# Seventh convolution pair moved into the in-projection's second part, with the work around the seam re-placed

## The chip, the cores and the metric

One core of a Trainium2 chip runs the program once. The metric is the device time of that run in microseconds (us).

## The reference, cut to what matters

One decoder layer on 1024 tokens of width 1024, all in float32. The change is inside the in-projection and what feeds on it:

```python
h = rms_norm(x, g_mix)
z = h @ w_in + b_in                              # 1024 -> 7168 columns
va, ga, xb, gb, sa, sb = split(z)                # 1024, 1024, 1536, 1536, 1024, 1024
u = causal_depthwise_conv(va * sigmoid(ga), conv_a_w, conv_a_b)     # width 31
y_a = silu(layer_norm(u)) @ w_a_out
v = rg_lru(causal_depthwise_conv(xb, conv_b_w, conv_b_b), ...)      # h[t] = a[t]*h[t-1] + b[t]
y_b = (v * gelu(gb)) @ w_b_out
x = x + (sigmoid(sa) * y_a + sigmoid(sb) * y_b) @ w_o
```

Then follow a squared-ReLU MLP and a last norm, which the change does not touch.

## The kernel before, in words

Every matmul is 128x128 by 128x512. To keep float32 accuracy each operand is split into a high part (rounded to the fast format) and a low part (what is left), and three products high*high, high*low, low*high are summed. The in-projection's 56 column chunks of 128 are done in two parts.

**First part (slots).** The list `CH` (line 704) holds 26 chunks: all 12 of `xb` and the pairs `va`/`ga` numbers 0 to 6. The loop over slots `s` (line 829) computes one chunk in each: 8 k-tiles x 3 products x 2 token halves = 48 matmuls (`chunk_mm`, L743). In between stand the small head matmuls `rg` (L550 to L552) of the recurrence's gates. Their results pass ScalarE as a sigmoid (L560) into head tiles `g15_0`, `g15_1`, and SyncE (SP) copies a third of the last head of each group of four into three gate tiles, `g0_9` to `g0_11` and `g1_9` to `g1_11` for the last group (L565). ScalarE then takes `exp` and `tanh` of each tile (`scan_exp`, L576 and L577) and a slot later a square root (`scan_root`, L584). [...] After the roots VectorE runs `scan_tile(t)` (L593 to L596): a scale, a one-column fill, a product and the recurrence scan itself; SP stores the result to `hd`.

**Second part (steps).** The remaining chunks are done in pairs by a seven-product scheme (Strassen-Winograd): two column blocks, two k halves, two token halves, and products numbered 1 to 7 over sums and differences of weights and of tokens. A product is 12 matmuls (`z_mm`, L944), a pair 84. `ZPAIRS` (line 747) lists the 15 pairs, `zseq` the order of the products; the first twelve steps are (pair, product) = (0,1) (1,1) (0,2) (1,2) (0,6) (0,7) (1,7) (0,5) (1,6) (0,3) (0,4) (1,5). Each product needs

- a weight operand `zo{pair}_{product}`, high and low, made four steps ahead (`z_lhs`): either ScalarE writes the high part and VectorE subtracts for the low part (products 5 and 7), or ScalarE writes the negated source, GpSimd (POOL) lets a DMA add the source to it for the low part, and ScalarE writes the high part (`split_dma`, L65 to L67); its source is a raw weight tile `zw` or a sum `zs` that VectorE makes;
- a token operand. Products 1 to 3 take the tokens of the first part. Products 4 to 7 take differences of token blocks: `x_load(c2)` reads the four blocks of k half `c2` back from DRAM, `x_sum(c2)` makes four subtractions on VectorE, `x_parts(c2, p)` splits the result for product `p` into `xs{p}h_{c2}` and `xs{p}l_{c2}`.

In each step the third matmul is the first that uses the low part of the weight operand. I call the border between the two parts the joint: the first matmul of step 0.

**Order.** All engines run their instructions in the order of the code inside `manual_schedule`; nothing is reordered. `later()` collects VectorE work of a slot or step and `vector_work` (line 718) sorts it by a modelled ready time and fills gaps with taps of the width-31 convolution (`conv`, L655) as far as a modelled clock allows. The dictionaries `XS` (line 818) and `ZX` (line 1036) say which token work stands in which slot or step. SP's DMA issues also stand in program order, and an issue that waits holds up all behind it.

Of the kernel before, what the change touches and what calls it, by code (L numbers as in the profile page):

```python
# [30 lines left out]
def trunk_kernel(ctx: ExitStack, tc: tile.TileContext, x, xt_in, xt_eo, vecs, w_in, w_a_out, w_b_pl, w_b_sq,  # L31
# [413 lines left out]
    VA, GA, XB, GB, SA, SB = 0, 8, 16, 28, 40, 48  # L445
# [121 lines left out]
    at_, rooted = {}, {}  # L567
# [23 lines left out]
    def scan_tile(t):  # L591
# [4 lines left out]
        nc.vector.tensor_tensor_scan(i, a, i, 0.0, ALU.mult, ALU.add)  # L596
        nc.sync.dma_start(hd[t], i)

    ut = {}
    yd = dp.tile([8, P, S], F32, name="yd")  # L600
    ysum = []
# [7 lines left out]
    def u_mul(j, ps, ready=0):  # L609
        uv = ut[j].rearrange("p (o n) -> p o n", o=2)  # L610
        later(ready, 1.28, nc.vector.scalar_tensor_tensor, uv, ps.rearrange("p (n o) -> p o n", o=2),
              bin_c[:, VA + j:VA + j + 1], uv, ALU.add, ALU.mult)
        fresh.append(j)
# [88 lines left out]
                      ALU.subtract)  # L702

    CH = [XB, VA, GA, XB + 1, XB + 2, VA + 1, GA + 1, XB + 3, XB + 4, XB + 5, VA + 2, GA + 2]
    CH += [XB + t for t in range(6, 12)] + [c for j in range(3, 7) for c in (VA + j, GA + j)]
    NU = 7
    CH[-2:] = CH[:-3:-1]
    NC1 = len(CH)
    zps = {n: z0[n] for n in range(N0)}
# [3 lines left out]
    def later(ready, cost, f, *a):  # L713

        todo.append((ready, len(todo), cost, f, a))

    def vector_work(end):
        for ready, _, cost, f, a in sorted(todo, key=lambda x: x[:2]):
            dve(cost, ready, f, *a)
        todo.clear()  # L720
        taps["wait"] += fresh
        fresh.clear()
        fill(end)
# [20 lines left out]
                                 start=n == 0, stop=n == 23)  # L744
        at("P", len(halves) * (n1 - n0) * MM)

    ZPAIRS = [GB + 2 * i for i in range(6)] + [VA + 7] + [SA + 2 * i for i in range(4)]
    ZPAIRS += [SB + 2 * i for i in range(4)]
    NZ = len(ZPAIRS)
    zraw, zs, zo, zb = {}, {}, {}, {}  # L750
    zn = [0]

    def z_load(i, kk):

        zraw[i, kk] = raw = qp.tile([P, 2, 4, P], F32, tag="p", name=f"zw{i}_{kk}", bufs=4)
        c = ZPAIRS[i]
        if c < GA:
# [51 lines left out]
    def z_get(n, f):  # L809
        return f(*zseq[n]) if 0 <= n < len(zseq) else None  # L810
# [4 lines left out]
    head_at = {s: n for n, s in enumerate(HS0)}  # L815

    EXP = {head_slot: g for g, head_slot in enumerate(HS0[4 * g + 3] + 1 for g in range(4))}
    XS = {NC1 - 5: ((x_load, 0),), NC1 - 4: ((x_sum, 0),), NC1 - 3: ((x_load, 1), (x_parts, 0, 6)),
          NC1 - 2: ((x_sum, 1), (x_parts, 0, 7, 5)), NC1 - 1: ((x_parts, 0, 4), (x_parts, 1, 6))}
    made = []  # L820
    head_w(0)
    w_load(3)
# [4 lines left out]
    with tc.manual_schedule(engines=ENGINES):  # L827
        for s in range(3, NC1):
# [30 lines left out]
            c = CH[s - 1]  # L859
# [27 lines left out]
            for d in range(5):  # L887
                if s - d in EXP:
# [6 lines left out]
                    t = 3 * g + d - (2 if g < 3 else 1)  # L895
                    if 3 * g <= t < 3 * g + 3:
                        later(rooted[t], 4.8, scan_tile, t)
            if s == NC1 - 1:
                z_get(0, z_lhs)
                z_get(1, z_lhs)  # L900
            for f, *a in XS.get(s, ()):
                f(*a)
# [48 lines left out]
    def z_u(i, j, m_, hf, src):  # L951

        if m_ and hf:
            return
        if (m_, hf) == (0, 0):
            uz[j] = T(f"u{j}")
        d = halved(uz[j], hf)
        if m_ == 0:
            nc.scalar.activation(d, src.rearrange("p (n o) -> p o n", o=2), AF.Sigmoid,
                                 bias=bin_c[:, GA + j:GA + j + 1])  # L960
            ready = at("A", 0.62)
            if hf == 0:
                return
            src = zb[i, "c"]
        else:
            ready = 0
        later(ready, 0.74, nc.vector.scalar_tensor_tensor, d,
              src.rearrange("p (n o) -> p o n", o=2), bin_c[:, VA + j:VA + j + 1], d,
              ALU.add, ALU.mult)
        if hf:  # L970
            ut[j] = uz.pop(j)
            fresh.append(j)

    def z_out(i, m_, hf, src, name):
        if ZPAIRS[i] < GA:
            z_u(i, ZPAIRS[i] - VA, m_, hf, src)
            return
        ci = ZPAIRS[i] + m_
        bias = bin_c[:, ci:ci + 1]
        if ci < SA:  # L980
            t = ci - GB
            h = hb.pop((t, hf))
            a = src if name else EV(f"ze{i}{m_}{hf}")
            nc.scalar.activation(a, src, AF.Gelu_apprx_tanh, bias=bias)

            def mult():
                nc.vector.tensor_tensor(h, h, a, ALU.mult)
                nc.sync.dma_start(hgd[t, :, HALVES[hf]], h)

            later(at("A", 0.62), 0.63, mult)  # L990
        else:
            b, j = divmod(ci - SA, 8)

            g = EV(f"zg{i}{m_}{hf}").rearrange("p (o n) -> p o n", o=2)
            nc.scalar.activation(g, src.rearrange("p (n o) -> p o n", o=2), AF.Sigmoid, bias=bias)
            at("A", 0.62)
            nc.sync.dma_start(halved(spill[b, j], hf), g)
# [35 lines left out]
        elif p == 4:  # L1033
            z_out(i, 1, 0, zb[i, "u"], "c")

    ZX = {0: ((x_parts, 1, 7),), 2: ((x_parts, 1, 5),), 4: ((x_parts, 1, 4),)}
    H_AT = {2: (0, 0), 5: (1, 1), 3: (0, 1), 4: (1, 0)}
    with tc.manual_schedule(engines=ENGINES):

# [118 lines left out]
        def b_post(i, x):  # L1158
# [16 lines left out]
            elif x == "11":  # L1175
# [4 lines left out]
        L = len(zseq)  # L1180
        ZX.update({L - 16: ((a_load, 0),), L - 13: ((a_sums, 0), (hb_load, 0, 0)),
                   L - 12: ((a_parts, 0, "a"), (hb_load, 0, 1)), L - 11: ((a_parts, 0, "s"), (hb_load, 1, 1)),
# [11 lines left out]
        z_get(3, z_lhs)  # L1194
        u_mul(NU - 1, zps[NC1 - 1])
        vector_work(clk["V"])
        z_h(0, 0, 0)
        for n in range(len(zseq) + 2):
            for f, *a in ZL.get(n, ()):
                f(*a)  # L1200
            if n >= L:
                for f, *a in ZX.get(n, ()):
                    f(*a)
# [4 lines left out]
            if n + 3 < len(zseq):  # L1208
                i, p = zseq[n + 3]
# [6 lines left out]
            if n < L:  # L1216
                for f, *a in ZX.get(n, ()):
                    f(*a)
# [751 lines left out]
    with tc.manual_schedule(engines={mybir.EngineType.Activation, mybir.EngineType.DVE,  # L1970
                                     mybir.EngineType.PE}):
        for n in range(len(useq)):
# [4 lines left out]
            while ready < min(len(useq), n + look + 1):  # L1977
                i, p = useq[ready]
# [316 lines left out]
```

## Time and profile before

| what | us |
|---|---|
| median of 3 runs (range) | 1529.34 (1529.16 to 1529.37) |
| the profiled execution | 1528.49 |
| its span on the core | 1526.7 |
| PE busy in the span | 1517.1 |
| VectorE, ScalarE busy | 1200.7, 928.1 |

The span runs from the first to the last instruction and is 1.8 us shorter than the execution's own time. PE is TensorE's matmul engine, DVE VectorE, ACT ScalarE, POOL GpSimd, SPq SyncE's queue of DMA issues. A row of the timeline has the start from the span's begin, the duration, engine, line, operation and tiles without their numbers; in square brackets stands the idle time before it and who ended it.

### The profile page before, as it was taken

To read this page: it belongs to the slowest core of one execution; us is meant where nothing else is said; L and a number is where in the kernel's file an instruction comes from. 1 tells how busy PE (TensorE), PEld (TensorE's weight loads), DVE (VectorE), ACT (ScalarE), POOL (GpSimd) and SP (SyncE) were. 2 spreads that over 40 slices of the span, in tenths; PEclk is the share of its full clock that TensorE was granted. 3 is DMA by queue.
4 is the path that set the end of the run, shared out by engine and by line. 5 is a ranking of instruction groups with operands and counts; after the bars stand their busy time and mean duration, and the time that the engine had idled before them with its cause. 6 is when DMAs were issued, how large, how long until landed. Compare 5 with 4: busy or idle time off the path is not lost.

```text
span 1526.7 us, 18955 instructions
## 1 busy us (share of the span) xinstructions
PE 1517.1 (99%) x6712; PEld 1248.3 (82%) x6712; DVE 1200.7 (79%) x1640; ACT 928.1 (61%) x1299; POOL 190.7 (12%) x228
## 2 busy tenths in 40 slices
PE   9999999999999999999999999999999999999998
PEld 7878887888888888888888888888888888888886
DVE  6999996999999997788769879755555387777777
ACT  6748688576566667645475777554444455545475
POOL 0111011022222222000022322000000000101010
PEclk9999999999999999999999999999999999999999
DMA  8757778698997789964779897333333974776464
GB/s 352 192 135 165 178 179 187 199 262 211 266 254 179 182 207 277 304 216 120 268 197 302 191 213 174 124 127 111 111 111 111 308 264 125 181 206 171 106 124 152
DMA packets 130911, 295.48 MB, mean 194 GB/s; under 512 B 12800, under 2 KB 34944, under 8 KB 130816
## 3 DMA queue, kind: packets, MB, share of 16 engines
q1 hardware_dynamic: 98960, 214.83, 41.5%
q0 software_dynamic: 31568, 78.92, 27.4%
q8 instruction: 52, 0.85, 0.2%
q10 hardware_dynamic: 288, 0.52, 0.1%
q14 instruction: 43, 0.35, 0.1%
HBM read 148.74 MB, written 60.82 MB: 137 GB/s over the span
## 4 chain that ended last, share of the span: by engine, by line
PE 99%; DMA 0%; DVE 0%; ACT 0%; SPq 0%; issue 0%
PE z L743 16%; PE d2b L2015 2%; PE d1b L2015 2%; PE d0b L2015 2%; PE z L273 2%; PE d3b L2015 2%; PE d0e L2015 1%; PE d3e L2015 1%; PE d3a L2015 1%; PE d2e L2015 1%; PE d1e L2015 1%; PE d1a L2015 1%; PE d0a L2015 1%; PE d2a L2015 1%; PE rg L550 1%; PE rg L552 1%
## 5 line engine op out<-in xcount | busy, mean ns | idle before, releaser
L743 PE MATMUL z<-xh,win_h 128*128 128x512 f32 x368 | 115.4, 391 | 0.0
L743 PE MATMUL z<-xl,win_h 128*128 128x512 f32 x368 | 114.9, 390 | 0.0
L655 DVE SCALAR_TENSOR_TENSOR y<-u,vec,y 128x511 f32<-128x511 f32 (+14 forms) x120 | 88.7, 739 | 0.0
L743 PE MATMUL z<-xh,win_l 128*128 128x512 f32 x368 | 87.5, 389 | 0.0
L655 DVE SCALAR_TENSOR_TENSOR yt<-u,vec,yt 128x511 f32<-128x511 f32 (+6 forms) x112 | 82.9, 740 | 0.0
L655 DVE SCALAR_TENSOR_TENSOR y<-yt,csum,y 128x511 f32<-128x511 f32 (+6 forms) x112 | 82.9, 740 | 0.0
L743 PEld LDWEIGHTS z<-xh,win_h 128*128 128x128 f32 x368 | 69.1, 188 | 16.0 <-ACT win_h L67 0.4
L743 PEld LDWEIGHTS z<-xl,win_h 128*128 128x128 f32 x368 | 69.1, 188 | 14.9
L743 PEld LDWEIGHTS z<-xh,win_l 128*128 128x128 f32 x368 | 69.1, 188 | 14.6
L560 ACT ACTIVATE g<-rg,vec 96x1024 f32<-96x1024 f32 x32 | 35.5, 1111 | 72.7 <-PE rg L552 72.7
L1710 ACT ACTIVATE o<-s 128x512 fp32r<-128x512 f32 x56 | 33.8, 624 | 45.2 <-DVE s L1694 26.4
L66 POOL DMA_DIRECT2D zo<-zw x45 | 38.9, 864 | 133.7 <-ACT zo L65 118.4
L501 DVE SCALAR_TENSOR_TENSOR v<-xb,vec,v 128x1023 f32<-128x1023 f32 (+2 forms) x36 | 46.2, 1282 | 4.4 <-ACT v L492 3.5
L66 POOL DMA_DIRECT2D db_10l<-br x4 | 3.5, 868 | 338.3 <-DMA br<-in_w_dram 253.1
L66 POOL DMA_DIRECT2D win_l<-win_raw x23 | 19.8, 861 | 190.6 <-ACT win_l L65 161.9
L65 ACT ACTIVATE zo<-zw 128x512 fp32r<-128x512 f32 x45 | 28.2, 627 | 24.3 <-PE z10f L944 2.1
L1234 DVE TENSOR_TENSOR o<-s,o 128x512 fp32r<-128x512 f32 x56 | 37.3, 684 | 1.5 <-ACT o L1710 1.5
L66 POOL DMA_DIRECT2D zo<-zs x30 | 26.1, 871 | 75.8 <-ACT zo L65 63.8
L67 ACT ACTIVATE zo<-zw 128x512 fp32r<-128x512 f32 x45 | 28.0, 622 | 0.0
L596 DVE TENSOR_TENSOR_SCAN g<-a,g 128x1024 f32<-128x1024 f32 x12 | 27.5, 2292 | 0.4
L66 POOL DMA_DIRECT2D ga<-gsa x8 | 6.9, 866 | 161.2 <-DMA m<-mbd 150.9
L1234 DVE TENSOR_TENSOR o<-w_raw,o 128x512 fp32r<-128x512 f32 x38 | 25.9, 685 | 0.0
(3178 smaller groups left out, 4908.2 us busy)
## 6 DMA issues: line engine op xcount, KB each, us to landing
w_raw<-in_w_dram SPq DMA_DIRECT2D x32, 512.0 KB, 5.5
br<-in_w_dram SPq DMA_DIRECT2D x32, 512.0 KB, 5.6
ar<-fd SPq DMA_DIRECT2D x32, 512.0 KB, 6.9
zw<-in_w_in_dram SPq DMA_DIRECT2D x28, 512.0 KB, 6.9
win_raw<-in_w_in_dram SPq DMA_DIRECT2D x23, 512.0 KB, 4.8
win_l<-win_raw POOLq DMA_DIRECT2D x23, 512.0 KB, 5.1
zo<-zw POOLq DMA_DIRECT2D x45, 256.0 KB, 5.7
gates<-zg SPq DMA_DIRECT2D x32, 256.0 KB, 4.5
```

Of the source, the lines that this page charges most:

```text
L65: nc.scalar.activation(l, src, AF.Copy, scale=-1.0)
L66: nc.gpsimd.dma_start(l, src, accum_op=ALU.add)
L67: nc.scalar.activation(h, src, AF.Copy)
L273: nc.tensor.matmul(z0[i][:, HALVES[hf]], w0[i][w][:, k, :], xpart(a, hf, k), start=k == 0 and which == "hh", stop=k == 7 and which == ("hl ...
L501: nc.vector.scalar_tensor_tensor(v[:, d:S], a[:, 0:S - d], cbw_c[:, w * 12 + t:w * 12 + t + 1], v[:, d:S], ALU.mult, ALU.add)
L560: nc.scalar.activation(a, gps.pop((n, gi))[:HD, :], AF.Sigmoid, bias=(ba_c, bx_c)[gi][:, n:n + 1])
L596: nc.vector.tensor_tensor_scan(i, a, i, 0.0, ALU.mult, ALU.add)
L655: nc.vector.scalar_tensor_tensor(o[:, k:], a[:, 0:HS - k], c, o[:, k:], ALU.mult, add)
L743: nc.tensor.matmul(zps[s][:, HALVES[hf]], w[:, k, :], xw[k][part][hf], start=n == 0, stop=n == 23)
L1234: tt(l, src, h.bitcast(F32), ALU.subtract)
L1710: nc.scalar.activation(o[:, 0], src, AF.Copy)
L2015: nc.tensor.matmul(o, a, b, start=start and n == 0, stop=stop and n == len(todo) - 1, skip_group_check=not start or not stop)
```

## The change

- `CH` loses `va`/`ga` pair 6: the first part has 24 slots instead of 26 (`NC1`), with conv pairs 0 to 5 (`NU` = 6).
- `ZPAIRS` gains that pair as fifth of 16 pairs (`VA + 6`), and `VA + 7` moves behind the last `gb` pairs.
- The token work counts from the end of the first part: the loads of half 0 stand two slots nearer to it, those of half 1 in the last slot. The four subtractions of half 1 and its split for product 6, and half 0's splits for products 5 and 4, stand behind the joint.
- The group of scan tiles 9 to 11 has two slots fewer: tile 9 stays in the last slot, 10 and 11 go to steps 2 and 3.
- The raw weights of the first two pairs (`zw`) are loaded in slot `NC1 - 3`, which is now slot 21 instead of 23.

```diff
+    def scan_later(t):
+        later(rooted[t], 4.8, scan_tile, t)
-    CH += [XB + t for t in range(6, 12)] + [c for j in range(3, 7) for c in (VA + j, GA + j)]
-    NU = 7
+    CH += [XB + t for t in range(6, 12)] + [c for j in range(3, 6) for c in (VA + j, GA + j)]
+    NU = 6
-    ZPAIRS = [GB + 2 * i for i in range(6)] + [VA + 7] + [SA + 2 * i for i in range(4)]
+    ZPAIRS = [GB + 2 * i for i in range(4)] + [VA + 6] + [GB + 8, GB + 10, VA + 7]
+    ZPAIRS += [SA + 2 * i for i in range(4)]
-    XS = {NC1 - 5: ((x_load, 0),), NC1 - 4: ((x_sum, 0),), NC1 - 3: ((x_load, 1), (x_parts, 0, 6)),
-          NC1 - 2: ((x_sum, 1), (x_parts, 0, 7, 5)), NC1 - 1: ((x_parts, 0, 4), (x_parts, 1, 6))}
+    XS = {NC1 - 3: ((x_load, 0),), NC1 - 2: ((x_sum, 0),), NC1 - 1: ((x_load, 1), (x_parts, 0, 6, 7))}
-    ZX = {0: ((x_parts, 1, 7),), 2: ((x_parts, 1, 5),), 4: ((x_parts, 1, 4),)}
+    ZX = {0: ((x_sum, 1), (x_parts, 1, 6)), 1: ((x_parts, 1, 7), (x_parts, 0, 5)), 2: ((scan_later, 10), (x_parts, 1, 5)), 3: ((x_parts, 0, 4),(scan_later, 11)),
+          4: ((x_parts, 1, 4),)}
```

**VectorE around the joint.** Before the change, VectorE's program from the row behind the last first-part multiplication (`u6`) to the low part of weight operand `zo0_5` of step 7 reads:

```order
L480 TENSOR_TENSOR xs7l_1_2838<-xs12_1_2600,xs7h_1_2837 128x1024
L480 TENSOR_TENSOR zs3_1_2858<-zw1_0_2614 128x512
L480 TENSOR_TENSOR zo0_7_2856<-zs3_0_2803,zo0_7_2856 128x512
L480 TENSOR_TENSOR zs4_0_2877<-zw0_1_2612,zs2_0_2802 128x512
L655 SCALAR_TENSOR_TENSOR y3_2334<-yt3_2335,csum_150,y3_2334 128x503
L655 SCALAR_TENSOR_TENSOR yt3_2335<-u3_2315,vec_89,yt3_2335 128x503
L480 TENSOR_TENSOR zo1_7_2875<-zs3_1_2858,zo1_7_2875 128x512
L480 TENSOR_TENSOR xs5l_1_2879<-xs11_1_2599,xs5h_1_2878 128x1024
L480 TENSOR_TENSOR zs1_1_2904<-zw1_0_2614,zw1_1_2616 128x512
L480 TENSOR_TENSOR zs2_1_2905<-zs1_1_2904,zw1_0_2614 128x512
L987 TENSOR_TENSOR hb0_0_2816<-hb0_0_2816,ze000_2888 128x512
L480 TENSOR_TENSOR zo0_5_2902<-zs1_0_2801,zo0_5_2902 128x512
```

Of the changed kernel these are two pieces of the same stretch. The first begins with the last first-part multiplication, now `u5`:

```order
L480 SCALAR_TENSOR_TENSOR u5_2595<-z23_2546,vec_89,u5_2595 128x1024
L480 TENSOR_TENSOR xs11_1_2608<-xs12_1_2609,xs11_1_2608 128x1024
L480 TENSOR_TENSOR xs12_1_2609<-xs22_1_2610,xs12_1_2609 128x1024
L480 TENSOR_TENSOR xs22_1_2610<-xs22_1_2610,xs11_1_2608 128x1024
L480 TENSOR_TENSOR xs21_1_2611<-xs21_1_2611,xs22_1_2610 128x1024
L480 TENSOR_TENSOR xs6l_1_2694<-xs22_1_2610,xs6h_1_2693 128x1024
L480 TENSOR_TENSOR zs3_1_2718<-zw1_0_2429 128x512
L480 TENSOR_TENSOR zo0_7_2716<-zs3_0_2659,zo0_7_2716 128x512
L480 TENSOR_TENSOR xs7l_1_2720<-xs12_1_2609,xs7h_1_2719 128x1024
L480 TENSOR_TENSOR zs4_0_2746<-zw0_1_2427,zs2_0_2658 128x512
```

The second follows directly behind the scale and the fill of scan tile 10 and holds the rest of that tile, tile 11 and the low part of `zo0_5`:

```order
L595 TENSOR_TENSOR g1_10_2322<-g0_10_2275,g1_10_2322 128x1024
L596 SCALAR_TENSOR_TENSOR g1_10_2322<-a10_2527,g1_10_2322 128x1024
L480 TENSOR_TENSOR zo1_7_2744<-zs3_1_2718,zo1_7_2744 128x512
L480 TENSOR_TENSOR xs5l_1_2748<-xs11_1_2608,xs5h_1_2747 128x1024
L480 TENSOR_TENSOR zs1_1_2776<-zw1_0_2429,zw1_1_2431 128x512
L480 TENSOR_TENSOR zs2_1_2777<-zs1_1_2776,zw1_0_2429 128x512
L593 SCALAR_TENSOR_TENSOR g0_11_2370<-a11_2530,g0_11_2370 128x1024
L594 MEMSET g0_11_2370 128x1
L595 TENSOR_TENSOR g1_11_2415<-g0_11_2370,g1_11_2415 128x1024
L596 SCALAR_TENSOR_TENSOR g1_11_2415<-a11_2530,g1_11_2415 128x1024
L990 TENSOR_TENSOR hb0_0_2672<-hb0_0_2672,ze000_2760 128x512
L480 TENSOR_TENSOR zo0_5_2774<-zs1_0_2657,zo0_5_2774 128x512
```

Four subtractions, the split `xs6l_1` and two scan tiles now stand between the joint and the low part of `zo0_5`, and the convolution's taps (L655) are gone from there. Ahead of the `u5` row stand, from the first root on: scan tile 9 with `zs1_0`, `zs2_0`, `zs3_0` between its parts, then `xs6l_0` and `xs7l_0`.

**SP's queue.** Before, the copies of the last head's gates (`g0_9` and on) stand between two loads of first-part weights; each row ends with the queues and engines that its issue waits for:

```order
L597 DMA hd_429<-g1_7_1900 128x1024 [waits DMAHW4_49]
L60 DMA win24_raw_2443<-in_w_in_dram 128x1024 [waits DMAHW5_49,DMASW3_49,Activation_49]
L565 DMA g0_9_2190<-g15_0_2470 32x1024 [waits Activation_49]
L565 DMA g0_10_2275<-g15_0_2470 32x1024 [waits DMAHW7_49]
L565 DMA g0_11_2370<-g15_0_2470 32x1024 [waits DMAHW0_49]
L565 DMA g1_9_2232<-g15_1_2513 32x1024 [waits DMAHW1_49,Activation_49]
```

In the changed kernel the four loads of `zw` stand ahead of them:

```order
L765 DMA zw0_0_2425<-in_w_in_dram 128x2x512 [waits DMAHW4_49]
L765 DMA zw0_1_2427<-in_w_in_dram 128x2x512 [waits DMAHW5_49]
L765 DMA zw1_0_2429<-in_w_in_dram 128x2x512 [waits PE_49]
L765 DMA zw1_1_2431<-in_w_in_dram 128x2x512 [waits DMAHW7_49,PE_49]
L597 DMA hd_429<-g1_7_1900 128x1024 [waits DMAHW0_49]
L565 DMA g0_9_2190<-g15_0_2476 32x1024 [waits DMAHW1_49,Activation_49]
L565 DMA g0_10_2275<-g15_0_2476 32x1024 [waits DMAHW2_49]
L565 DMA g0_11_2370<-g15_0_2476 32x1024 [waits DMAHW3_49]
L565 DMA g1_9_2232<-g15_1_2519 32x1024 [waits DMAHW4_49,Activation_49]
```

The two loads of `zw1` reuse the buffers of the last head's tokens (`vh15`, `vl15`), so their wait on PE ends with the last `rg` matmuls; the gate copies now stand behind that wait.

**ScalarE.** Between the last `tanh` and the first weight operand of the second part ScalarE's program of the changed kernel reads (`u5` is the sigmoid of `ga` 5, the L584 rows are the roots of tiles 9 to 11):

```order
L577 ACTIVATE g0_11_2370<-g0_11_2370,sm_149 128x1024
L608 ACT_TABLE_LOAD
L608 ACTIVATE u5_2595<-z22_2451,vec_89 128x1024
L584 ACT_TABLE_LOAD
L584 ACTIVATE g0_9_2190<-g0_9_2190 128x1024
L584 ACTIVATE g0_10_2275<-g0_10_2275 128x1024
L584 ACTIVATE g0_11_2370<-g0_11_2370 128x1024
L65 ACTIVATE zo0_1_2600<-zw0_0_2425 128x512
```

Before, the split of `win24` stood in the place of the first table load and `u5`, and between the roots and `zo0_1` stood the splits of half 0's tokens for products 6, 7 and 5, a table load, `u5`, the split of `win25` and `u6`. The token splits of half 0 now follow `zo0_1` and `zo1_1`, the weight splits are gone with their chunks.

## The prediction

> **What bounds the kernel now.** I begin with the page: the span, the engines' busy time and the shares of the chain that ended last.
>
> ```profile
> span 1526.7 us, 18955 instructions
> PE 1517.1 (99%) x6712; PEld 1248.3 (82%) x6712; DVE 1200.7 (79%) x1640; ACT 928.1 (61%) x1299; POOL 190.7 (12%) x228
> PE 99%; DMA 0%; DVE 0%; ACT 0%; SPq 0%; issue 0%
> ```
>
> TensorE is busy all the time and carries the whole chain. The view of waits, kept to PE, says how often it stood still:
>
> ```profile
> PE z L273 <- ACT xh L235: 1.3, 1, 1.3
> PE spare L360 <- POOL ones L108: 1.0, 1, 1.0
> ```
>
> There are two waits, both in the first 7 us of the program. At the joint there is none. So the time is the number of matmuls times their spacing, and a matmul less is a gain only as long as everything that PE waits for stays early. The chain in order of time gives the spacing on both sides of the joint:
>
> ```profile
> 300.60 38.13 PE z L743 x168
> 338.73 2.72 PE z0a L944 x12
> ...
> 357.76 2.72 PE z0e L944 x12
> ```
>
> A first-part matmul takes 38.13 / 168 = 0.227 us, a product of twelve 2.72.
>
> **What the change saves on PE.** Two slots of 48 matmuls go: 96 x 0.227 = 21.8. One pair of seven products comes: 7 x 2.72 = 19.0. That is 12 matmuls and **2.75 us less**, if PE waits nowhere. It is under 0.2% of the time (3 us, about what a measurement of this kernel can tell from no change). All else turns on the seam, which now lies 21.8 earlier: on the clock of the profile before at 338.56 - 21.8 = **316.8**, by the first of these rows. The others show when step 7, product (0,5), comes to its third matmul, the first that reads the low part of `zo0_5`:
>
> ```profile
> 338.56 0.39 PE L944 MATMUL z0a<-xh,zo 128*128 128x512 f32 x1
> ...
> 357.60 0.39 PE L944 MATMUL z0e<-xs5h,zo 128*128 128x512 f32 x1
> 358.06 0.61 PE L944 MATMUL z0e<-xs5h,zo 128*128 128x512 f32 x2
> ```
>
> That is 358.06 - 338.56 = 19.5 us behind the joint, so without a stall PE asks for it at 316.8 + 19.5 = 336.3.
>
> **When ScalarE can give the first root.** The last gates end at the same time as before, since the slots up to 22 stay. From there ScalarE ran:
>
> ```profile
> 300.64 1.12 ACT L560 ACTIVATE g<-rg,vec 96x1024 f32<-96x1024 f32 x1 [2.84 <-PE rg L552]
> 301.77 1.28 ACT L576 ACT_TABLE_LOAD   x1
> 303.07 1.16 ACT L576 ACTIVATE a<-g,c 128x1024 f32<-128x1024 f32 x1
> ...
> 309.77 1.04 ACT L65 ACTIVATE win_l<-win_raw 128x1024 fp32r<-128x1024 f32 x1
> ...
> 313.08 2.96 ACT L584 ACTIVATE g<-g 128x1024 f32<-128x1024 f32 x3
> ...
> 320.49 1.12 ACT L605 ACTIVATE u<-z,vec 128x1024 f32<-128x1024 f32 x1
> ```
>
> The six `exp` and `tanh` took 309.77 - 303.07 = 6.7. The table load waits for the copy `g0_9`, which had landed long before. Now SP holds that copy behind the loads `zw1`, whose wait ends with the `rg` matmuls at 300.6. The views of the two lines of SP, the gate copies (L565) and the `zw` loads (L761), end with the times to landing:
>
> ```profile
> L565 SPq DMA_DIRECT2D g<-g x6: 507/548/587, 294.9 to 303.0; - x6
> DMA to landing us min/median/max: 2.2/2.3/2.5
> ```
>
> ```profile
> L761 SPq DMA_DIRECT2D zw<-in_w_in_dram x4: 439/454/646, 307.9 to 309.7; - x4
> DMA to landing us min/median/max: 12.5/13.4/14.5
> ```
>
> Two `zw1` and one store `hd`, about 0.5 each, come first, so the copy is issued at about 302.3. Alone it lands 2.3 later, at 304.6. But the landings of the four `zw` lie (309.7 + 14.5) - (307.9 + 12.5) = 3.8 apart from first to last, 1.3 each: big loads land one behind another. With three of them ahead, 2.3 + 3 x 1.3 = 6.2 after the first issue at 300.7, the copy lands at **307**, which I take; 304.6 is the early end. Then 1.3 for the table, 6.7, a table and `u5` (1.28 + 1.12), the root's table (1.28) and the first of three roots (2.96 / 3): that is 12.7, and the first root is there at 307 + 12.7 = **319.7**, at the early end 317.3. With no delay of the copy at all it would be 301.77 + 12.7 = 314.5.
>
> This alone makes PE wait: ScalarE turns to `zo0_1`, the weights of step 0, after two more roots, at 321.7, and its low part needs a DMA:
>
> ```profile
> L66 POOL DMA_DIRECT2D zo<-zw x4: 862/862/862, 331.6 to 337.6; - x4
> DMA to landing us min/median/max: 3.2/6.6/7.8
> ```
>
> 321.7 + 0.6 for the negated copy + 0.3 to POOL's issue + 3.2 is 325.8, 9 us behind the joint. It is covered by a longer lateness, though, that of VectorE.
>
> **VectorE's chain.** Scan tile 9 waits for the first root, and VectorE takes its program in order. These are its durations at the seam before:
>
> ```profile
> 320.15 4.99 DVE L480 TENSOR_TENSOR xs<-xs,xs 128x1024 f32<-128x1024 f32 x4
> 325.06 1.22 DVE L593 SCALAR_TENSOR_TENSOR g<-a,g 128x1024 f32<-128x1024 f32 x1
> ...
> 329.90 1.26 DVE L480 SCALAR_TENSOR_TENSOR u<-z,vec,u 128x1024 f32<-128x1024 f32 x1
> 331.08 1.21 DVE L480 TENSOR_TENSOR xs7l<-xs,xs7h 128x1024 fp32r<-128x1024 f32 x1
> 332.21 1.22 DVE L593 SCALAR_TENSOR_TENSOR g<-a,g 128x1024 f32<-128x1024 f32 x1
> ...
> 344.22 0.69 DVE L480 TENSOR_TENSOR zs<-zw,zs 128x512 f32<-128x512 f32 x1
> 344.83 0.73 DVE L655 SCALAR_TENSOR_TENSOR y<-yt,csum,y 128x503 f32<-128x503 f32 x1
> ...
> 349.80 0.68 DVE L480 TENSOR_TENSOR zo<-zs,zo 128x512 fp32r<-128x512 f32 x1
> ```
>
> From start to start, a scan tile takes 329.90 - 325.06 = 4.84, the four token subtractions 4.9, `u` 1.2, a low part of tokens 1.13, a 512-wide operation 0.61 to 0.69. From the first root to the low part of `zo0_5` now stand three scan tiles (14.5), the subtractions (4.9), `u5` (1.2), five token lows (5.65) and eleven 512-wide ones (0.63 each, 6.9): **33.1 us**. Before, that low part was done at 349.80 + 0.68 = 350.5, 7.6 early: the subtractions and scan tiles 10 and 11, from 320.15 to 332.21 + 4.84, lay under matmuls of the two slots that go. That cover is gone, and only two taps (the L655 row and its neighbour) stood in this stretch that could make room.
>
> So `zo0_5` is ready at 319.7 + 33.1 = 352.8, and PE wants it at 336.3: **16.5 us late**. The early end of the copy gives 14.1, no delay 11.3. Other operands are late by less: `zo1_7`, some 9 us further up the chain, is wanted 2.7 earlier, so its lateness is 6 less; `zo1_6` comes 6 us ahead of `zo0_5` but then needs ScalarE, a place in POOL's queue and a landing of 3.2 to 7.8, and is wanted 2.7 later, so it is 0 to 5 less late. Behind step 7 the spacing of the work is that of before, VectorE has no taps there until it has caught up, and PE, which waits for no one now, has no stall to give the lateness back to.
>
> **The restart.** PE idles for several us before step 7. The program's start shows what its first matmuls cost after rest:
>
> ```profile
> 1.00:3.90 2.90, 2.90 (x13) 2.90 (x14) 1.00 0.67 191
> 3.90:5.00 1.10, 1.03 (x9) 0.84 (x7) 1.00 1.07 382
> 6.19 0.50 PE L273 MATMUL z<-xh,w_h 128*128 128x512 f32 x1 [1.26 <-ACT xh L235]
> ```
>
> The first 13 small matmuls take 2.9 us, the next come about twice as fast, so some 1 to 1.4 is lost; after the 1.26 us pause the spacing was full at once. The cost here lies between 0 and 1.4; the idle time is long, as at the start, so I take **1**, the low side of that row.
>
> [...]
>
> **The sum.** 16.5 + 1 - 2.75 = +14.75. Against the profiled execution (1528.49, with 1.8 of it around the span) that is 1543.2; the median of the runs is 0.85 above it, so **1544.1 us**. The other edits I cost at nothing: ScalarE's extra table loads for the `va` 6 pair among the `gelu` steps follow the pattern of `va` 7's before, and those made no PE wait; the convolution's end moves nearer to the layer norm, but its last sum had long reserves, as the view of the tile `ysum` from 580 to 640 us shows. Without that cover each would cost a few us.
>
> ```profile
> L668 POOL DMA_DIRECT2D ysum<-y x1: 1212/1212/1212, 586.5 to 586.5; - x1
> L1251 ACT ACTIVATE mu1h<-ysum x1: 615/615/615, 638.7 to 638.7; 128x512 fp32r<-128x512 f32 x1
> DMA to landing us min/median/max: 9.7/9.7/9.7
> ```
>
> The sum lands at 596.2 and is read at 638.7, so the convolution may end 40 us later at no cost.
>
> **Rivals.**
>
> - *The copies land as early as before*, because the queue is not what holds them. The first root comes at 314.5, the operand 11.3 late: 11.3 + 1 - 2.75 = +9.55, 1538.9; without a slow restart 1537.9. Against it stands SP's row with its wait for PE. Chance 0.17.
> - *The landings pile up.* POOL's DMAs took up to 7.8 here, and behind a stalled seam `zo1_6`, `zo0_3` and the later `zw2` loads, which SP holds behind the stores of scan tiles 10 and 11, come late too: 3 to 6 us more, 1547 to 1550. Chance 0.18.
> - *The vector work is early enough and the 12 matmuls are all that counts.* The mechanism is VectorE's head start: if scan tile 9 could start 16.5 us earlier than I work out, at 303.2, `zo0_5` would be there when PE asks for it, and the time would be 1529.34 - 2.75 = 1526.6. With a lateness below 2.75 the kernel is not slower. For it speaks that VectorE kept 7.6 us of reserve before; against it that the last gates end at 300.6 and 12.7 us of ScalarE follow the copy. Chance 0.04.
> - My forecast: 0.61.
>
> The range takes in the first two rivals' nearer ends: 1537.5 to 1549.5. Slower by over 0.2% holds all cases but the third, 0.95; the third is 0.18% below, so it is split: same 0.03, faster 0.02.
>
> **What would show it.** In the changed profile PE's waits at the seam: one for POOL's `zo` at step 0 of about 9 us, later ones for VectorE's low parts of `zo`, the last at the first matmuls of `z0e`; together 16 to 17. The table load ahead of `exp` would stand behind a landing at about 307. The distance from the first root to the low part of `zo0_5` should be 33 us. The matmuls right behind the last wait should be spaced wider than 0.227. I am wrong if PE's waits sum to under 10 or if a wait ends behind step 8.

## The result, and the profile after

The changed kernel takes **1552.27 us** (median of 4 runs, 1551.18 to 1552.82) beside 1529.25 for the kernel before on the same chip: a ratio of **1.0155, 95% interval 1.0142 to 1.0167**. The forecast was 1544.1, with a range of 1537.5 to 1549.5: the direction is right, the size is not, and the time lies outside the range. The profiled execution took 1552.26, its span 1550.5. From its page, the engines' busy time, PE in 40 slices and the chain that ended last:

```profile
PE 1523.4 (98%) x6700; PEld 1251.3 (81%) x6700; DVE 1205.8 (78%) x1649; ACT 937.3 (60%) x1316; POOL 192.6 (12%) x231
PE   9999999978999999999999999999999999999998
PE 92%; DMA 3%; DVE 2%; issue 1%; ACT 1%; SPq 0%; POOL 0%; POOLq 0%; ACTq 0%; DVEq 0%
```

The 12 matmuls are gone (6712 before), yet PE's busy time is 6 us longer: its matmuls were slower somewhere. The chain, which was PE alone, now leaves PE for DMA, VectorE and ScalarE, in the two slices around 310 to 390 us that show 7 and 8. The view of waits, kept to PE, gives the places behind the program's start (engine, tile, line, what was waited for; total, times, longest):

```profile
PE z0a L947 <- ACT zo L67: 7.4, 1, 7.4
PE z0e L947 <- DVE zo L480: 2.7, 1, 2.7
PE z0e L947 <- ACT z0e L1016: 2.0, 1, 2.0
PE z0a L947 <- DMA zo<-zw: 1.8, 1, 1.8
PE z6e L947 <- DMA zo<-zs: 1.3, 1, 1.3
PE z14f L947 <- DMA zo<-zw: 1.2, 1, 1.2
...
PE z3e L947 <- DMA zo<-zs: 0.9, 1, 0.9
...
PE z15e L947 <- DMA zo<-zs: 0.5, 1, 0.5
PE z15e L947 <- ACT zc L1024: 0.4, 1, 0.4
```

The four rows of `z0a` and `z0e` are the seam, 13.9 us. The other five stand far behind step 8, where the prediction had no wait.

The seam as ScalarE saw it, in its timeline (start, duration, and in brackets the idle time before it and what ended that), with the landing of the gate copies from the view of SP's line:

```profile
300.41 1.11 ACT L560 ACTIVATE g<-rg,vec 96x1024 f32<-96x1024 f32 x1 [2.85 <-PE rg L552]
308.25 1.28 ACT L576 ACT_TABLE_LOAD   x1 [6.72 <-DMA g<-g]
...
320.08 2.95 ACT L584 ACTIVATE g<-g 128x1024 f32<-128x1024 f32 x3
```

```profile
L565 SPq DMA_DIRECT2D g<-g x6: 520/596/1659, 302.0 to 306.6; - x6
...
DMA to landing us min/median/max: 4.4/5.3/6.3
```

The last gate ends at 301.5, and the table load waits till 308.25 for the first copy, which was issued at 302.0 and took 6.3 to land. The three roots begin at 320.08 and take 2.95; the first is done at about 321.1.

VectorE's chain, from scan tile 9 to the low part of `zo0_5`:

```profile
321.17 1.23 DVE L593 SCALAR_TENSOR_TENSOR g<-a,g 128x1024 f32<-128x1024 f32 x1 [2.39 <-ACT g L584]
...
353.41 0.69 DVE L480 TENSOR_TENSOR zo<-zs,zo 128x512 fp32r<-128x512 f32 x1
```

It runs from 321.17 to 353.41 + 0.69 = 354.1, 32.9 us. And PE behind the wait for it:

```profile
354.15 1.22 PE L947 MATMUL z0e<-xs5h,zo 128*128 128x512 f32 x2 [2.69 <-DVE zo L480]
355.17 0.63 PE L947 MATMUL z0e<-xs5l,zo 128*128 128x512 f32 x1
355.59 1.05 PE L947 MATMUL z0e<-xs5h,zo 128*128 128x512 f32 x2
...
360.29 0.40 PE L947 MATMUL z1b<-xs6l,zo 128*128 128x512 f32 x1
360.53 0.63 PE L947 MATMUL z1b<-xs6h,zo 128*128 128x512 f32 x2
```

The starts lie 0.427 apart (355.17 to 355.59) up to 360.29, and 0.23 from there on.

For all kernels below I add up, from the timeline of PE, by how much the starts of neighbouring matmuls lie over 0.227 apart, wherever they are over 0.245. In the changed kernel that is 18.0 up to 354.15 (14.7 at the four waits and 3.2 in slow matmuls behind those of step 0), 3.0 for the slow matmuls behind 354.15, and **5.6 behind the seam** (1.2 at 423.5, 1.6 at 482.3, 1.5 at 630.6, 1.4 at 641.8 and 643.0). In the kernel before it is 0.03 over the same steps; what follows them has 0.4 in both. 26.6 - 2.7 for the 12 matmuls = 23.9, where the spans differ by 23.8.

### The profile page after: what moved, and what is told of

Same layout as the page of the kernel before. It is cut to its first block, busy times and chain, and to the rows that moved or that the text cites. A ratio compares the mean times of both kernels' runs of the same rounds, so it can differ in the third digit from the quotient of the medians.

```text
span 1550.5 us, 18984 instructions
## 1 busy us (share of the span) xinstructions
PE 1523.4 (98%) x6700; PEld 1251.3 (81%) x6700; DVE 1205.8 (78%) x1649; ACT 937.3 (60%) x1316; POOL 192.6 (12%) x231
## 4 chain that ended last, share of the span: by engine, by line
PE 92%; DMA 3%; DVE 2%; issue 1%; ACT 1%; SPq 0%; POOL 0%; POOLq 0%; ACTq 0%; DVEq 0%
PE z L746 14%; PE d2b L2019 2%; PE d1b L2019 2%; PE d0b L2019 2%; PE z L273 2%; DMA zo<-zs 2%; PE d0e L2019 1%; PE d3b L2019 1%; PE d3e L2019 1%; PE d2e L2019 1%; PE d2a L2019 1%; PE d1e L2019 1%; PE d1a L2019 1%; PE d0a L2019 1%; PE d3a L2019 1%
## 5 line engine op out<-in xcount | busy, mean ns | idle before, releaser
L746 PE MATMUL z<-xh,win_h 128*128 128x512 f32 x336 | 105.6, 392 | 0.0
L746 PE MATMUL z<-xl,win_h 128*128 128x512 f32 x336 | 105.2, 390 | 0.0
L746 PE MATMUL z<-xh,win_l 128*128 128x512 f32 x336 | 79.9, 390 | 0.0
L746 PEld LDWEIGHTS z<-xh,win_h 128*128 128x128 f32 x336 | 63.1, 188 | 14.7 <-ACT win_h L67 0.4
L746 PEld LDWEIGHTS z<-xl,win_h 128*128 128x128 f32 x336 | 63.1, 188 | 13.6
L746 PEld LDWEIGHTS z<-xh,win_l 128*128 128x128 f32 x336 | 63.1, 188 | 13.3
L65 ACT ACTIVATE zo<-zw 128x512 fp32r<-128x512 f32 x48 | 30.0, 625 | 26.2 <-PE z1f L947 2.1
L67 ACT ACTIVATE zo<-zw 128x512 fp32r<-128x512 f32 x48 | 29.8, 620 | 0.0
```

What stands on the lines that cost most here:

```text
L65: nc.scalar.activation(l, src, AF.Copy, scale=-1.0)
L67: nc.scalar.activation(h, src, AF.Copy)
L746: nc.tensor.matmul(zps[s][:, HALVES[hf]], w[:, k, :], xw[k][part][hf], start=n == 0, stop=n == 23)
```

## The experiments

Each is the changed kernel with one or more differences. "Seam" is the sum just described from the joint to the end of the slow matmuls behind step 7 (or step 10, in the one kernel where a wait there ends it), "behind" what comes later up to the product stage.

| kernel | us | ratio to before, 95% | seam | behind |
|---|---|---|---|---|
| changed kernel | 1552.27 | 1.0142 to 1.0167 | 21.0 | 5.6 |
| e1_sum_later | 1548.72 | 1.0117 to 1.0148 | 21.1 | 2.0 |
| e2_loads_behind | 1545.02 | 1.0085 to 1.0119 | 13.1 | 8.0 |
| e3_scan_later | 1551.04 | 1.0131 to 1.0161 | 15.9 | 9.2 |
| e4_keep_busy | 1550.73 | 1.0128 to 1.0158 | 18.0 | 6.3 |
| e5_both | 1541.67 | 1.0075 to 1.0108 | 13.0 | 2.1 |
| e6_three | 1540.06 | 1.0059 to 1.0089 | 11.6 | 4.1 |
| e7_weights_first | 1542.69 | 1.0077 to 1.0107 | 14.9 | 1.9 |
| e8_all | 1539.12 | 1.0053 to 1.0084 | 11.5 | 2.4 |
| e9_no_y7 | 1539.33 | 1.0053 to 1.0083 | 14.3 | 0.0 |
| f1_filler | 1561.38 | 1.0195 to 1.0229 | 8.4 | 4.8 |
| f2_filler_sum | 1558.58 | 1.0178 to 1.0208 | 9.5 | 2.0 |

My theory for the missing 8 us: the seam is as I worked it out, only a little longer, and the waits behind it are due to the places that the convolution's accumulates now have in POOL's order. The rival: they are an echo of the seam, since ScalarE and VectorE run behind from there on.

**e1_sum_later**

```diff
-            nc.gpsimd.dma_start(ysum[0], acc, accum_op=add)
+            held.append(acc)
+            if not taps["z"]:
+                y_add()
...
             z_get(n + 4, z_lhs)
+            if n + 5 >= len(zseq) or zseq[n + 5][1] == 5:
+                y_add()
```

> The changed kernel with one difference: in the in-projection's second part POOL issues the five accumulates of the convolution's sum (ysum, from y3 to y7) behind the low part of a product 3 and ahead of a product 1, where most of them stood before the change; no other engine's order differs. The changed kernel lost 5.6 us at five places behind the seam (423.5, 482.3, 630.6, 641.8 and 643.0 us). Theory: there a low part of zo stands right behind a 512 KB accumulate in POOL's queue and lands behind it, so the new order takes these stalls away: 1552.3 - 5.6 = 1546.7, seam unchanged. Rival: the low parts are late because ScalarE and VectorE still run behind from the seam, or because the DMA engines are full: the stalls stay or move, 1551 to 1553.

The first late wait in the changed kernel: the low part of `zo3_3` in POOL's timeline, the time to landing in the view of its line, and the view of the accumulate that POOL issued 2.8 us earlier:

```profile
413.34 0.87 POOL L66 DMA_DIRECT2D zo<-zs  x1 [1.57 <-ACT zo L65]
```

```profile
DMA to landing us min/median/max: 10.1/10.1/10.1
```

```profile
L671 POOL DMA_DIRECT2D ysum<-y x1: 1228/1228/1228, 410.6 to 410.6; - x1
...
DMA to landing us min/median/max: 11.1/11.1/11.1
```

The accumulate lands at 421.7 and the low part at 423.4, just when PE goes on (the wait of `z3e` above). In e1_sum_later the two are exchanged. The accumulate in its timeline, and the low part in the view of its line:

```profile
414.24 1.24 POOL L680 DMA_DIRECT2D ysum<-y  x1
```

```profile
L66 POOL DMA_DIRECT2D zo<-zs x1: 877/877/877, 413.7 to 413.7; - x1
...
DMA to landing us min/median/max: 6.7/6.7/6.7
```

6.7 instead of 10.1, and nobody waits. Of the 5.6 us, the four waits for landings are all but gone (5.0 with what follows each); 2.0 stay or come anew where the part ends, 1.3 of them a wait of `yb0b` for ScalarE. The time falls by 3.5, of 5.6 expected. The order in POOL's queue is shown as the cause of the landings; whether the DMA engines serve the two one behind the other or share them is not told apart by this. Such landings were there before the change too: one low part that POOL issued at 538.8 in the kernel before, 1.4 behind an accumulate, took 9.5 to land, and PE waited for nothing. What the change moved is which low part stands there, and how soon PE needs it.

**e2_loads_behind**

```diff
             if s == NC1 - 3:
-                for i in range(4):
-                    z_load(i // 2, i % 2)
+                for i in range(2):
+                    z_load(0, i)
+            if s == NC1 - 2:
+                for i in range(2):
+                    z_load(1, i)
```

> The changed kernel with the two loads of zw1 one slot later in SP's queue, behind the six gate copies instead of ahead of them. Theory: the loads' wait for the rg matmuls is what holds the copies; without them the copy g0_9 is there when ScalarE has ended the last gate, the 6.7 us that ScalarE idled ahead of the table load go, the first root comes at about 314.4 instead of 321.1, and the wait at step 7 shrinks by the same: 1552.3 - 6.7 = 1545.6. Rival: the copies are held by something else (the gates themselves, or the landing), and ScalarE idles as before: 1552. In between: the copies land 2 to 4 us earlier, 1548 to 1550.

Measured: 7.2 us less, near the 6.7 of the theory. In the profiled execution, the slowest of the four, the seam is 7.9 shorter, and the waits behind it are 2.4 longer, for which I have no cause. The copies and ScalarE:

```profile
L565 SPq DMA_DIRECT2D g<-g x6: 507/546/582, 295.0 to 303.0; - x6
...
DMA to landing us min/median/max: 2.2/2.3/2.4
```

```profile
301.83 1.28 ACT L576 ACT_TABLE_LOAD   x1
...
313.67 2.96 ACT L584 ACTIVATE g<-g 128x1024 f32<-128x1024 f32 x3
```

The copies are issued from 295.0 again and land in 2.3, the table load follows the last gate without a pause, and the roots start 6.4 earlier. Both halves of the prediction's step hold: the queue held the copies (issued from 302.0 in the changed kernel), and with the two loads of `zw1` just ahead of them they landed slowly, in 4.4 to 6.3 us instead of 2.2 to 2.4 here.

**e3_scan_later**

```diff
-    ZX = {..., 2: ((scan_later, 10), (x_parts, 1, 5)), 3: ((x_parts, 0, 4),(scan_later, 11)), 4: ((x_parts, 1, 4),)}
+    ZX = {..., 2: ((x_parts, 1, 5),), 3: ((x_parts, 0, 4),), 4: ((x_parts, 1, 4), (scan_later, 10)), 5: ((scan_later, 11),)}
```

> The changed kernel with scan tiles 10 and 11 two slots later, so that on VectorE they stand behind the low part of zo0_5 instead of ahead of it. Theory: VectorE's chain from the first root sets the seam; it gets 2 x 4.85 = 9.7 shorter, and step 7 is then no longer what PE waits for longest. Left is the wait of step 0 for POOL's low part of zo0_1 with the slow matmuls behind it, 12.9 us in all in the changed kernel, instead of 21.0: 1552.3 - 8.1 = 1544.2. Rival: the low part of zo1_6 or of zo0_3, which pass through ScalarE and POOL, is late by nearly as much, and the scan tiles then delay the next operands: a gain of 0 to 4, 1548 to 1552.

The seam shrinks by 5.1, not by 8.1. VectorE has the low part of `zo0_5` 9 us earlier, at 344.9 by its timeline, but ScalarE's timeline shows another wait in its place:

```profile
347.45 1.06 ACT L67 ACTIVATE xs4h<-xs 128x1024 fp32r<-128x1024 f32 x1 [2.88 <-DVE g L595]
...
351.10 0.58 ACT L1016 ACTIVATE z0e<-z0b 128x512 f32<-128x512 f32 x1
```

```profile
344.21 0.69 DVE L480 TENSOR_TENSOR zo<-zs,zo 128x512 fp32r<-128x512 f32 x1
...
346.19 1.22 DVE L595 TENSOR_TENSOR g<-g,g 128x1024 f32<-128x1024 f32 x1
```

`xs4h` and scan tile 10 share nothing but the pool: `xs4h` takes a buffer that the tile's multiplication (L595) sets free. A scan tile moved later therefore holds ScalarE, and the copy into `z0e` queues behind it. Behind the seam the loss grows to 9.2, most of it one wait of 2.9 for the low part of `zo6_3` with the restart behind it; with the accumulates moved (e6_three) that wait is gone. Why it was longer here than in the changed kernel I leave open. In all the kernel gains 1.2; the intervals overlap, so the reading rests on the trace and not on the time.

**e4_keep_busy**

```diff
+                if (i, p) == (0, 5) and n in KEEP:
+                    for d in range(KEEP[n]):
+                        nc.tensor.matmul(zb[0, "a"], xbh[1][0][:, d * P:(d + 1) * P], xbh[1][0][:, 0:HS], ...)
                 nc.tensor.matmul(ps, a, b_, ...)
...
+    KEEP = {0: 8, 2: 8}
```

> The changed kernel with 8 matmuls that nobody reads ahead of the first and 8 ahead of the third matmul of step 7, into a bank whose content is no longer needed; they fill 1.8 us of each of the two idle stretches there (2.4 and 3.1 us from start to start). Theory: the 14 matmuls that took 0.427 instead of 0.227 behind the last wait of the seam are slow because PE had idled; with the idle time filled the slow stretch goes and nothing else changes: 1552.3 - 3.0 = 1549.3. Rival: the spacing of 0.427 comes from something else (weights or tokens that arrive late, the DMA traffic): 1552, with the slow stretch still there.

PE's timeline behind the same wait:

```profile
353.96 0.73 PE L953 MATMUL z0e<-xs5h,zo 128*128 128x512 f32 x2 [0.81 <-DVE zo L480]
354.54 0.40 PE L953 MATMUL z0e<-xs5l,zo 128*128 128x512 f32 x1
354.77 0.62 PE L953 MATMUL z0e<-xs5h,zo 128*128 128x512 f32 x2
```

The wait ends at the same time (353.96), but the matmuls behind it are 0.23 apart at once. The seam costs 18.0 (the 16 added matmuls counted in it), 3.0 less as expected, so the slow stretch is the price of having idled. The time falls by only 1.5, with overlapping intervals: the waits behind the seam give back 0.7, and one of 0.9 us comes up much later in the program (`d0a`, for VectorE).

**e5_both, e6_three, e7_weights_first, e8_all.** e5_both holds the edits of e1 and e2, e6_three those of e1, e2 and e3. e7_weights_first is e5_both with

```diff
-            if s == NC1 - 1:
+            if s == NC1 - 2:
                 z_get(0, z_lhs)
                 z_get(1, z_lhs)
```

and e8_all is that with scan tiles 10 and 11 at steps 4 and 5 and `x_parts(0, 4)`, `x_parts(1, 4)` at 5 and 6.

> The two differences of e1_sum_later and e2_loads_behind together. Theory: they are terms of different places (the queue of POOL behind step 8, the queue of SP ahead of the joint) and add up. With the loads behind the copies PE lost 13.1 us to the end of the seam, with the accumulates later 2.4 behind it: 15.5 instead of the 27.0 of the changed kernel, 1552.3 - 11.5 = 1540.8. Rival: one takes from the other what it had gained, since a PE that is earlier meets the landings of the next low parts: 1543 to 1545, no faster than e2_loads_behind.

> e5_both with scan tiles 10 and 11 behind the low part of zo0_5 as in e3_scan_later. In e3_scan_later VectorE's low part of zo0_5 was early, but ScalarE's copy into z0e came late, because xs4h ahead of it in ScalarE's order waited 2.9 us for a buffer that scan tile 10 sets free. Theory: the first root is 6.7 earlier here, so that copy is 15.8 - 6.7 = 9.1 late and is the last wait of the seam; 9.5 at the seam and 2.4 to 5 behind it: 1537 to 1540. Rival: VectorE alone sets the seam, which then ends with step 1 at 7.7: 1535.5.

> e5_both with the weights of steps 0 and 1 (four short operations of ScalarE, 2.1 us) ahead of the roots instead of behind them. PE's wait of 5.3 us at step 0 goes. Theory: that wait was covered by the one at step 7, which VectorE's chain from the first root sets; the root comes 2.1 later, so step 7 waits till 11.4 + 2.1 = 13.5 behind its time, in one piece, and the restart behind so long a pause costs the full 3.0: 16.5 at the seam instead of 13.1, slower than e5_both by 3.4, about 1544. Rival: the wait of step 0 counts by itself, and taking it away is a gain: 1537 or less.

> e7_weights_first with scan tiles 10 and 11 behind the low part of zo0_5, and the parts of xs4 two slots later, so that ScalarE's copy into z0e no longer stands behind a buffer of scan tile 10. Theory: step 7 waits for VectorE by 13.5 - 9.7 = 3.8, with 0 to 3 for the restart, and 2.4 are lost behind the seam; against the kernel before that is 3.8 + 1.5 + 2.4 - 2.75 = +5, about 1533.5. Rival: the later xs4 or the later scan tiles make steps 10 and 11 or the products of pair 6 wait: 1537 to 1541.

e5_both: the two terms add up, 15.4 in all with 15.5 expected. e6_three: the copy into `z0e` ends the seam, as expected (PE waited 2.0 for it), with a slow stretch of 1.4 behind it that I had not counted: 1540.06, just above the range. e7_weights_first: no gain (its interval is nearly that of e5_both; its traced losses are 1.7 larger), so a wait that a later one covers is worth nothing by itself. The size that I expected for the loss, 3.4, was too large. e8_all falls short: 1539.1 and not 1533.5. Step 7 waits no longer, but four other waits at the seam take its place:

```profile
PE z0a L957 <- DMA zo<-zw: 2.2, 2, 1.2
...
PE z0f L957 <- DVE zc L480: 1.9, 1, 1.9
PE z1a L957 <- ACT z1b L1023: 1.7, 1, 1.7
PE z0a L957 <- ACT z0b L1023: 1.2, 1, 1.2
```

No version came near the kernel before.

**e9_no_y7**

```diff
-            held.append(acc)
+            if j < 7:
+                held.append(acc)
```

> e5_both without the accumulate of y7, the last channel tile of the convolution, so that the layer norm's mean lacks it. In e1_sum_later, e5_both and the kernels built on it PE lost about 2 us where the second part ends (z15e, yb0b), behind ScalarE, which waited there for the loads hg. Theory: the convolution now ends 33 us later than before the change, and a load hg waits for the buffer of y7 until its accumulate has landed; without the accumulate the loads start about 8 us earlier and these 1.9 us go: 1541.7 - 1.9 = 1539.8, and PE's waits behind the seam are under 0.3. Rival: the loads wait for other buffers or for the DMA engines, and the wait for ScalarE at z15e or yb0b stays at 1 to 2 us: 1541.7.

This asks for the 2 us where the part ends, in the kernels with the accumulates moved. The kernel leaves `y7` out of the convolution's sum. In e8_all's view of the loads `hg` the second is issued at 621.1, 8 us behind the first, and the accumulate of `y7` was issued at 610.6 and took 10.5: it lands at 621.1. That the load waits for the buffer of `y7` is read from these two times.

```profile
L1058 SPq DMA_DIRECT2D hg<-hgd x2: 320/456/592, 621.1 to 621.8; - x2
```

```profile
L680 POOL DMA_DIRECT2D ysum<-y x1: 1207/1207/1207, 610.6 to 610.6; - x1
...
DMA to landing us min/median/max: 10.5/10.5/10.5
```

Without that accumulate PE waits nowhere behind the seam, the second load follows the first by 0.9 us (616.9 and 617.8), and ScalarE's wait of 4.0 for `hg` in e5_both is gone. 1539.33 with 1539.8 expected.

**f1_filler and f2_filler_sum**

```diff
+                fill_ps = PS("zf")
+                for n in range(48):
+                    for hf in (0, 1):
+                        nc.tensor.matmul(fill_ps[:, HALVES[hf]], wst[s][0][:, n % 8, :], xw[n % 8][0][hf], ...)
```

> The changed kernel with 96 matmuls that nobody reads ahead of the joint, as many as stood in the two slots that the change takes out (21.8 us). Theory: the seam's waits are lost cover alone, and the late waits come from POOL's order and not from the seam. Then PE waits nowhere at the seam, and the late waits stay at about 5.6: against the kernel before there is one pair more (84 x 0.227 = 19.05) and 5.6, 1528.4 + 24.7 = 1553.1, about the time of the changed kernel with 21.8 us more work for PE. Rival: the late waits are an echo of the seam, and go with it: 1547.5.

> f1_filler with the accumulates of the convolution's sum later in POOL's order, as in e1_sum_later. Theory: no waits at the seam, and behind it only the 1 to 2 us where the second part ends: 1528.4 + 19.05 + 1.5 = 1549, 4 less than f1_filler. Rival: with the seam mended nothing is left for the order in POOL's queue to cure, and both take the same.

On the waits behind the seam the theory holds: they stay at 4.8 with a seam of 8.4 instead of 21.0, and fall to 2.0 with the accumulates moved. They do not shrink with the seam, so they are no echo of it. On the seam the theory failed: I expected no wait, and 8.4 remained, so that the kernels are 8 and 10 slower than expected. VectorE's timeline of f1_filler shows why:

```profile
339.65 0.69 DVE L480 TENSOR_TENSOR zs<-zw,zw 128x512 f32<-128x512 f32 x1 [9.88 <-PE zf L907]
```

VectorE stood for 9.9 us at the first weight sum, until PE had ended the added matmuls. The sum takes nothing from them; by the code its pool opens where that of the first part's weights closes, and the added matmuls read the last slot's weights to their end, so a shared buffer is the likely reason. In its fixed order the token sums of the second half and scan tiles 10 and 11 come behind it, some 14 us of work that in the kernel before was done ahead of the joint. In the changed kernel this limit did not bind, since the first root came later than the joint. In the kernel before, the same sum began 0.4 ahead of the joint (338.56) and waited for nobody:

```profile
338.17 0.69 DVE L480 TENSOR_TENSOR zs<-zw,zw 128x512 f32<-128x512 f32 x1
```

So the added matmuls hold VectorE in a way that two real slots did not, and what such slots ahead of the joint would make of the seam is not shown.

## Why the prediction was wrong, point by point

- *The saving and the joint* (2.75 less, joint at 316.8): right. The last matmul of the first part leaves the joint at 316.6.
- *The copies held in SP's queue* (landing at 307, first root at 319.7): the mechanism is right and shown by e2_loads_behind; they landed 1.2 later, and the root came 1.4 later.
- *VectorE's chain of 33.1 us*: right, 32.9. PE asked for `zo0_5` at 316.6 + 19.5 = 336.1 and got it at 354.1, **18.0 late, not 16.5**. That it ended the seam is shown by e3_scan_later: with 9.7 less of it another wait took over.
- *Step 0's wait, covered*: right, about 9 as forecast. 7.4 and 1.8 us were waited there, and 3.2 lost in slow matmuls behind them. The forecast had not counted these, but step 7's wait covers them as well. Taking step 0's wait away (e7_weights_first against e5_both) gained nothing.
- *"The cost here lies between 0 and 1.4 ... so I take 1"*: wrong in size. The restart cost **3.0**, shown by e4_keep_busy (18.0 at the seam instead of 21.0). I read the cost from the program's start, where the 13 slow matmuls, small ones, lasted 2.9 us in all; here the slow stretch, 14 matmuls 0.427 apart, lasted 6.1 us.
- *"PE, which waits for no one now, has no stall to give the lateness back to"*, with nothing behind step 8, and *the convolution's end at no cost*: **the step that failed.** I looked at the layer norm, the reader of `ysum`, and there the reserve was real. But each of the convolution's accumulates is also a place in POOL's queue and a buffer of the pool. The last one was issued at 619.7, 33 us later than the 586.5 of before, and landed 9.0 later, at 628.7:

```profile
L671 POOL DMA_DIRECT2D ysum<-y x1: 859/859/859, 619.7 to 619.7; - x1
```

  Three of them came to stand directly ahead of a low part of `zo` that PE needed soon (423.5, 482.3 and 630.6). These are 4.2 of the 5.6 us, and e1_sum_later, f1_filler and f2_filler_sum show the queue as their cause. The other 1.4, at 641.8 and 643.0, have a longer way. VectorE stood still ahead of `hb1l`, up to 629.2, and ScalarE stood still for VectorE, by the views of their waits:

```profile
DVE hb1l L480 <- DMA gates<-zg: 7.1, 1, 7.1
```

```profile
ACT hb7h L1053 <- DVE hb L480: 5.5, 1, 5.5
```

  So the last low part, for `z15e`, left POOL only at 635.9 and landed at 642.9. The view names a store of `gates`, but that landed at 630.4, after the wait had ended. The last accumulate landed 0.5 ahead of its end, and in e2_loads_behind the same wait (7.6) is put down to `ysum<-y`; so this too looks like the buffer of `y7`, read from the trace and not tested in the changed kernel. e9_no_y7 shows that buffer as a cause for the loads `hg`, in the kernels with the accumulates moved.
- *The rival of 1547 to 1550* ("the landings pile up") had the right kind and nearly the right size, but named `zo1_6`, `zo0_3` and the loads `zw2`. PE waited for none of them.

The sum then reads 18.0 + 3.0 + 5.6 - 2.75 = 23.85, where the forecast had 14.75 and the spans differ by 23.8. The term that stood at nothing, 5.6, is the largest part of the 9.1 between them; the restart has 2.0 and the later operand 1.5.

## What to carry to other kernels

Where work is taken from the engine that sets the time, list all that ran under it, and ask of each piece not only when it can start but behind which instruction its engine's order now puts it, and whose buffer it waits for. When a chain of work ends later, look at every queue that its DMAs stand in, not only at the reader of its result. And of several late operands only the latest counts: the next ones lie close below it, so mend them in the order of time and expect less than the wait that goes.

## What the runs showed of the hardware that was not expected

**When a pause slows TensorE down.** Pauses of about the same length cost nothing or up to 3 us. By the starts of the matmuls, PE idled 3.03 us in e3_scan_later, up to 351.73, and went on with starts 0.34 and 0.24 apart and then 0.23; in e8_all it idled 2.05, up to 353.54, and the next eight were 0.427 apart. First e3_scan_later, then e8_all:

```profile
351.73 0.50 PE L947 MATMUL z0e<-xs5h,zo 128*128 128x512 f32 x1 [2.87 <-ACT z0e L1016]
352.07 0.40 PE L947 MATMUL z0e<-xs5l,zo 128*128 128x512 f32 x1
352.31 0.62 PE L947 MATMUL z0e<-xs5h,zo 128*128 128x512 f32 x2
```

```profile
353.54 0.63 PE L957 MATMUL z0f<-xs4h,zo 128*128 128x512 f32 x1 [1.89 <-DVE zc L480]
353.96 0.63 PE L957 MATMUL z0f<-xs4l,zo 128*128 128x512 f32 x1
354.39 1.05 PE L957 MATMUL z0f<-xs4h,zo 128*128 128x512 f32 x2
```

The wait that ended at 354.15 in the changed kernel (2.69 by the view of waits) was followed by 6.1 us at a spacing of 0.427, which is the 3.0 lost. The granted clock, as a share of full speed, was 0.50 there from 354.15 to 360.29, and 1.00 from then to 366. Another wait in the same run (1.99, up to 350.73) was followed by a start 0.33 later. So the length of a pause alone does not tell what it costs. e4_keep_busy took the pause away; what else decides its cost was not shown, since no run tried the length or the place of a pause by itself.

**A DMA behind a large accumulate.** A low part of 256 KB that POOL issued 2.8 us behind a 512 KB accumulate landed in 10.1 us, and in 6.7 when it was issued 0.5 ahead of it.
